# Channel-major weight products of a hybrid decoder trunk: rows' upper and lower parts in one 512-column matmul

## The chip, the cores and the metric

The kernel runs on one core of one Trainium2 chip. The metric is the time of one execution in device microseconds; before the change it is 1853.26 us, the median of three runs (1852.25 to 1854.35). Lower is better. Only matrix and vector work of one core is involved; there are no collectives.

## The reference, cut to what matters

Two decoder layers act on 256 rows of 1024 channels. Each layer has a token mixer (an RWKV-7 group of 8 heads and a native-sparse-attention group of 8 heads behind one input projection, then one output projection), a 4-head cross-attention into 256 memory rows, and a SwiGLU channel mixer: dense in layer 0, top-2 of 8 experts in layer 1. All arithmetic is float32.

```python
def rmsnorm(x, g):
    xf = x.astype(jnp.float32)
    y = xf * lax.rsqrt(jnp.mean(xf * xf, -1, keepdims=True) + NORM_EPS)
    return (y * g).astype(x.dtype)

def token_shift(u, mu):
    prev = jnp.pad(u, ((0, 0), (1, 0), (0, 0)))[:, :-1]
    return u + (prev - u) * mu

def cross_attention(h, m, wq, wkv, wo):
    q = (h @ wq).reshape(B, T, CROSS_HEADS, CROSS_HEAD_DIM)
    kv = (m @ wkv).reshape(B, M, 2, CROSS_HEADS, CROSS_HEAD_DIM)
    ...

def swiglu(h, wg, wu, wd):
    return (jax.nn.silu(h @ wg) * (h @ wu)) @ wd
```

The products that matter here are `h @ w` with h of 256 rows by 1024 channels: the mixer's input projection, the cross-attention's queries and keys, and the dense layer's gate and up products.

## The kernel before, in words

To keep float32 accuracy on the matrix engine, each operand is split into an upper part (rounded to the type float32r) and a lower part (what is left). A product is then three matmuls: upper by upper, lower by upper, upper by lower. Weights are split on the fly by `split` (L382 on ScalarE makes `wh`, L383 on VectorE makes `wl`), 128 by 1024 values at a time, into three rotating buffers in the mixers and more elsewhere.

`proj_b` (L396 to L410) makes channel-major results: 128 output channels on the partitions, 256 rows along the free dimension. A **tile** of weights from memory (1 MB, `raw`) has two **blocks** of 128 channels. For a block, the loop over 8 groups of input channels issues L405 (`wh` by the rows' upper part `hh`), L406 (`wh` by the lower part `hl`) and L407 (`wl` by `hh`), each 256 columns wide, all adding into one half of a PSUM bank. Both blocks of a tile share one bank, and the evicting function `evac` is called once for a tile. There are 120 blocks in the kernel, so 960 of each of the three matmuls:

- the mixer's RWKV columns, `proj_rwkv`, 14 blocks a layer; each block is evicted by `shift`, one ScalarE instruction (L580) and one VectorE instruction (L581) that both read PSUM;
- the mixer's attention columns, `proj_nsa`, 8 blocks a layer (`ev_c`, `ev_k`, `ev_q`);
- the memory's keys, `mem_kv`, 8 blocks a layer;
- the cross-attention's queries, `cross`, 8 blocks a layer;
- the dense layer's gate and up products, `dense`, 44 blocks. Here the results stay in PSUM until `second` multiplies them by 1 / rms (L1220, L1228).

`proj_a` (L424 to L426), `out_proj`, the dense down products (L1244 to L1246) and the experts (L1589 to L1591, L1628 to L1630) work row-major, with the weights as the 512-column moving operand; the change leaves them alone.

What sets the order of the work: each engine runs its own list of instructions, fixed when the program is built, by the order in the source, by readiness in the planner's estimate of times, and by a few edges written by hand (`behind`, `hold`, `chained`). In the mixer `weave` interleaves two lists of steps, RWKV's and the attention's with the memory's keys and values, by costs given with each `yield`. The PSUM banks of the tag `pj`, into which `proj_b` writes, are two in the mixer, three in the cross-attention and four in the dense layer. The experts (from about 850 us on) are written out in order by hand.

Of the kernel before, what the change touches and what calls it, by code (L numbers as in the profile page):

```python
# [14 lines left out]
D = 1024  # L15
# [20 lines left out]
M0 = 2, 1  # L36
# [121 lines left out]
def weave(*gens):  # L158
    """Steps of several generators, given as (generator, cost of all its steps), at an even pace."""
# [16 lines left out]
class Trunk:  # L176
# [37 lines left out]
    # constants  # L214
    def consts(self):
# [48 lines left out]
        # rows of a half of 32 in its second 16 and columns in its first  # L264
# [16 lines left out]
        # a pair of heads' sums go to rows 32 j and 32 j + 1, and to the two after those, which keep their lower parts  # L281
# [53 lines left out]
    # weights  # L335
# [24 lines left out]
    def extra(self, ctx, nraw, nspl, side=None):  # L360
        """Further buffers for the weights until ctx ends."""
# [34 lines left out]
    def proj_b(self, src, hh, hl, evac, tag="pj", m=128):  # L396
        """src [n, 128, 2, 8, 128]: channel-major blocks; evac(first block, psum [128, 2, 256])."""
        nc = self.nc
        for n in range(src.shape[0]):
            w, self.early = self.early or self.raw(src[n]), None  # L400
            ps = self.bank3(tag, 2)
            for b in range(2):
                wh, wl = self.split(w[:, b])
                for k in range(8):
                    nc.tensor.matmul(ps[:, b], wh[:, k], hh[:, k], start=(k == 0), stop=False)  # L405
                    nc.tensor.matmul(ps[:, b], wh[:, k], hl[:, k], start=False, stop=False)  # L406
                    nc.tensor.matmul(ps[:, b], wl[:, k], hh[:, k], start=False, stop=(k == 7))  # L407
# [41 lines left out]
    def rms(self, src, pool, junk, name="rs", both=False):  # L449
        """1 / rms of the rows: [128, 2]; junk [128, >= 512] is written over. Squares by ACT, or by DVE too."""  # L450
# [23 lines left out]
    def behind(self, ins, name):  # L474
        """The engine issues ins after the other of its instructions."""
# [1229 lines left out]
```

## Time and profile before

| | us |
|---|---|
| time, median of three runs | 1853.26 (1852.25 to 1854.35) |
| profiled execution, first to last instruction (span) | 1849.4 |
| median time less that span | 3.9 |
| TensorE busy in the span | 1808.4 |
| VectorE busy | 1461.3 |
| ScalarE busy | 1219.6 |

The profiled execution is one more execution; the page gives its span and not a time of its own, so the 3.9 us that lie around the span are taken from the median of the runs. In the rows, PE is TensorE's matmuls, PEld its weight loads, DVE VectorE, ACT ScalarE, POOL GpSimd. The end of a matmul is modelled, so the duration of one (283 ns for 256 columns) holds its latency; what a matmul costs in a stream is the distance from its start to the start of the next one.

### The profile page before, as it was taken

The page shows a single profiled execution, that of the slowest core. Times are in us where ns is not written, and L with a number is a line of the kernel's source. Part 1 is how long each engine was busy: PE and PEld are TensorE (multiplying, and loading weights), DVE is VectorE, ACT ScalarE, POOL GpSimd, SP SyncE. Part 2 cuts the span into 40 slices and gives each one's busy share as a digit, 9 for nine tenths or more (in the row PEclk, how much of TensorE's full clock was granted, in tenths as well). Part 3 has the DMA queues.
Part 4 walks back from the last instruction along what each step waited for, and adds up shares of the span by engine and source line. Part 5 has one row for each costly group of instructions (what it writes and reads, how often), then busy time and mean ns, then how long its engine had stood idle before and what let it go on. Part 6 is the DMA issues. An engine that isn't in the chain of part 4 may idle for free.

```text
span 1849.4 us, 28947 instructions
## 1 busy us (share of the span) xinstructions
PE 1808.4 (98%) x11309; PEld 1514.4 (82%) x11309; DVE 1461.3 (79%) x1947; ACT 1219.6 (66%) x1632; POOL 68.3 (4%) x152
## 2 busy tenths in 40 slices
PE   9999999999999999999999999999999999999997
PEld 9886788999988877877888788888888888888885
DVE  6777475655568774748999899998999999999997
ACT  7654354544466644448778677777777878777776
POOL 3100000000001100010000000000000000000000
PEclk9999999999999999999999999999999999999999
DMA  6532163555244421758998799998999989999990
GB/s 233 177 143 70 47 261 129 177 186 182 69 138 159 139 92 47 284 218 317 364 352 330 272 350 351 368 362 321 369 358 362 369 319 365 363 356 369 356 358 27
DMA packets 66674, 467.28 MB, mean 253 GB/s; under 512 B 7377, under 2 KB 7505, under 8 KB 11745
## 3 DMA queue, kind: packets, MB, share of 16 engines
q1 hardware_dynamic: 66208, 464.79, 68.5%
q8 instruction: 90, 1.47, 0.3%
q10 hardware_dynamic: 288, 0.52, 0.1%
q14 instruction: 56, 0.45, 0.1%
q0 software_dynamic: 32, 0.03, 0.0%
HBM read 464.27 MB, written 1.05 MB: 252 GB/s over the span
## 4 chain that ended last, share of the span: by engine, by line
PE 90%; DVE 5%; ACT 3%; issue 1%; DMA 0%; SPq 0%; ACTq 0%; DVEq 0%
PE gu L1591 11%; PE gu L1590 11%; PE gu L1589 11%; PE y L1629 6%; PE y L1628 6%; PE y L1630 6%; PE pj L405 6%; PE pj L406 6%; PE pj L407 6%; DVE wl L383 2%; PE pj L424 1%; PE pj L426 1%; PE pj L425 1%; PE tr L1605 1%; PE acc L1244 1%; PE acc L1245 1%
## 5 line engine op out<-in xcount | busy, mean ns | idle before, releaser
L383 DVE TENSOR_TENSOR wl<-raw,wh 128x1024 fp32r<-128x1024 f32 (+1 forms) x846 | 1019.7, 1218 | 191.2 <-ACT wh L382 185.0
L382 ACT CAST wh<-raw 128x1024 fp32r<-128x1024 f32 (+1 forms) x848 | 877.2, 1040 | 420.1 <-PE pj L406 142.2
L1589 PE MATMUL gu<-wh,xe 128*128 128x512 f32 x896 | 356.5, 398 | 0.0
L1591 PE MATMUL gu<-wh,xe 128*128 128x512 f32 x896 | 354.1, 395 | 0.0
L1590 PE MATMUL gu<-wl,xe 128*128 128x512 f32 x896 | 351.9, 393 | 0.0
L406 PE MATMUL pj<-hl,wh 128*128 128x256 f32 x960 | 276.3, 289 | 3.4 <-DVE hl L446 3.4
L407 PE MATMUL pj<-hh,wl 128*128 128x256 f32 x960 | 274.7, 287 | 1.4 <-DVE wl L383 1.4
L405 PE MATMUL pj<-hh,wh 128*128 128x256 f32 x960 | 275.3, 288 | 0.6 <-DVE gl L581 0.4
L1591 PEld LDWEIGHTS gu<-wh,xe 128*128 128x128 f32 x896 | 168.1, 188 | 38.5
L1590 PEld LDWEIGHTS gu<-wl,xe 128*128 128x128 f32 x896 | 168.6, 188 | 37.8
L1589 PEld LDWEIGHTS gu<-wh,xe 128*128 128x128 f32 x896 | 168.4, 188 | 35.6
L406 PEld LDWEIGHTS pj<-hl,wh 128*128 128x128 f32 x960 | 186.8, 195 | 6.1 <-DVE hl L446 4.5
L405 PEld LDWEIGHTS pj<-hh,wh 128*128 128x128 f32 x960 | 186.0, 194 | 4.5 <-issue 2.0
L407 PEld LDWEIGHTS pj<-hh,wl 128*128 128x128 f32 x960 | 186.8, 195 | 2.5 <-DVE wl L383 1.9
L1629 PE MATMUL y<-wl,hth 128*128 128x512 f32 x448 | 177.8, 397 | 2.4 <-DVE wl L383 2.4
L1628 PE MATMUL y<-wh,hth 128*128 128x512 f32 x448 | 178.4, 398 | 0.0
L1630 PE MATMUL y<-wh,htl 128*128 128x512 f32 x440 | 174.4, 396 | 0.0
L1629 PEld LDWEIGHTS y<-wl,hth 128*128 128x128 f32 x448 | 84.6, 189 | 22.7 <-DVE wl L383 2.9
L1628 PEld LDWEIGHTS y<-wh,hth 128*128 128x128 f32 x448 | 84.7, 189 | 19.9
L1630 PEld LDWEIGHTS y<-wh,htl 128*128 128x128 f32 x440 | 83.1, 189 | 20.1
L1601 DVE SCALAR_TENSOR_TENSOR h<-gu,gs,h 128x512 f32<-128x512 f32 x56 | 41.7, 744 | 1.7 <-ACT wh L382 0.9
L1065 ACT ACTIVATE pn<-pn,mx 128x128 f32<-128x128 f32 x64 | 28.5, 447 | 16.1 <-DVE mx L1062 15.7
(515 smaller groups left out, 2119.9 us busy)
## 6 DMA issues: line engine op xcount, KB each, us to landing
raw<-eg SPq DMA_DIRECT2D x106, 1024.0 KB, 5.1
raw<-eu SPq DMA_DIRECT2D x104, 1024.0 KB, 5.0
raw<-ed SPq DMA_DIRECT2D x104, 1024.0 KB, 5.2
raw<-win SPq DMA_DIRECT2D x21, 1024.0 KB, 4.9
raw<-dg SPq DMA_DIRECT2D x11, 1024.0 KB, 4.8
raw<-du SPq DMA_DIRECT2D x11, 1024.0 KB, 4.8
raw<-dd SPq DMA_DIRECT2D x11, 1024.0 KB, 4.8
raw<-ck SPq DMA_DIRECT2D x8, 1024.0 KB, 4.8
```

The costliest lines, as they stand in the source:

```text
L382: nc.scalar.copy(wh[:, c], w[:, c])
L383: (low or nc.vector).tensor_sub(wl[:, c], w[:, c], wh[:, c].bitcast(F32))
L405: nc.tensor.matmul(ps[:, b], wh[:, k], hh[:, k], start=(k == 0), stop=False)
L406: nc.tensor.matmul(ps[:, b], wh[:, k], hl[:, k], start=False, stop=False)
L407: nc.tensor.matmul(ps[:, b], wl[:, k], hh[:, k], start=False, stop=(k == 7))
L1589: nc.tensor.matmul(ps, xe[0][:, k + kk, es], wh[:, kk], start=(k + kk == 0), stop=False)
L1590: nc.tensor.matmul(ps, xe[0][:, k + kk, es], wl[:, kk], start=False, stop=False)
L1591: nc.tensor.matmul(ps, xe[1][:, k + kk, es], wh[:, kk], start=False, stop=(k + kk == 7))
L1601: nc.vector.scalar_tensor_tensor(h, gu[1], rs, h, op0=ALU.mult, op1=ALU.mult)
L1628: nc.tensor.matmul(ys[o], hh[:, k], wh[:, c], start=st, stop=False)
L1629: nc.tensor.matmul(ys[o], hh[:, k], wl[:, c], start=False, stop=False)
L1630: nc.tensor.matmul(ys[o], hl[:, k], wh[:, c], start=False, stop=sp)
```

## The change

Rows are held in one tile `hx` with the upper and the lower part of a channel group next to each other, 2 by 256 columns. In `proj_b` one 512-column matmul multiplies `wh` by both parts, and one of 256 columns multiplies `wl` by the upper part, into the first half of the bank. A block now fills a whole PSUM bank: its first half holds two of the three products, its second half the third. `evac` is called for every block, and the halves are added on the way out: `both` copies one half by ScalarE and adds the other by VectorE. What used to read PSUM afterwards (`shift`, the multiplications by 1 / rms) reads the result in SBUF. The hunks left out drop comments, follow the renaming, and join the two buffers `m1` and `m2` of the last layers into one of twice the size, `m12`.

```diff
-    def proj_b(self, src, hh, hl, evac, tag="pj", m=128):
-        """src [n, 128, 2, 8, 128]: channel-major blocks; evac(first block, psum [128, 2, 256])."""
+    def proj_b(self, src, hx, evac, tag="pj"):
...
             w, self.early = self.early or self.raw(src[n]), None
-            ps = self.bank3(tag, 2)
             for b in range(2):
+                ps = self.bank3(tag, 2)
                 wh, wl = self.split(w[:, b])
                 for k in range(8):
-                    nc.tensor.matmul(ps[:, b], wh[:, k], hh[:, k], start=(k == 0), stop=False)
-                    nc.tensor.matmul(ps[:, b], wh[:, k], hl[:, k], start=False, stop=False)
-                    nc.tensor.matmul(ps[:, b], wl[:, k], hh[:, k], start=False, stop=(k == 7))
-                if b:
-                    evac(2 * n, ps)
+                    nc.tensor.matmul(ps.rearrange("p a t -> p (a t)"), wh[:, k], hx[:, k].rearrange("p a t -> p (a t)"),
+                                     start=(k == 0), stop=False)
+                    nc.tensor.matmul(ps[:, 0], wl[:, k], hx[:, k, 0], start=False, stop=(k == 7))
+                evac(2 * n + b, ps)
                 yield 2.6

+    def both(self, dst, ps, scale=1.0):
+
+        self.nc.scalar.activation(dst, ps[:, 1], AF.Copy, scale=scale)
+        self.nc.vector.scalar_tensor_tensor(dst, ps[:, 0], scale, dst, op0=ALU.mult, op1=ALU.add)
+
...
-        hh = self.rw.tile([128, 8, 256], F32R, name="hh")
-        hl = self.rw.tile([128, 8, 256], F32R, name="hl")
+        hx = self.rw.tile([128, 8, 2, 256], F32R, name="hx")
+        hh, hl = hx[:, :, 0], hx[:, :, 1]
...
-        def ev_w(b, ps):
-            self.shift(ps[:, 0], 12, self.wa)
-            self.shift(ps[:, 1], 13, self.gl)
-
         def ev(dst, o):
             def f(b, ps):
-                for q in range(2):
-                    self.shift(ps[:, q], o + b + q, dst[:, b + q])
+                self.both(dst(b), ps)
+                self.shift(dst(b), o + b, dst(b))
             return f
...
-        def ev_c(b, ps):
-            for s in range(2):
-                for g in range(2):
-                    sl = slice(64 * g, 64 * g + 64)
-                    copy = nc.vector.tensor_copy if s else nc.scalar.copy
-                    copy(self.kv2[s][0:64, g], ps[sl, s])
-                    copy(self.kv2[s][64:128, g, 0:255], ps[sl, s, 1:256])
+        def ev_c(s, ps):
+            for g in range(2):
+                sl = slice(64 * g, 64 * g + 64)
+                for d, p in ((self.kv2[s][0:64, g], ps[sl]), (self.kv2[s][64:128, g, 0:255], ps[sl, :, 1:256])):
+                    nc.scalar.copy(d, p[:, 1])
+                    nc.vector.tensor_add(d, d, p[:, 0])

         def ev_k(b, ps):
-            nc.scalar.copy(self.ks[:, 16:272], ps[:, 0])
-            nc.scalar.copy(self.kw, ps[:, 1])
+            self.both(self.kw if b else self.ks[:, 16:272], ps)

         def ev_q(b, ps):
-            for i in range(2):
-                nc.scalar.activation(self.q[:, b + i], ps[:, i], AF.Copy, scale=self.qs[:, b + i:b + i + 1])
...
+            self.both(self.q[:, b], ps, self.qs[:, b:b + 1])
...
         def ev_k(b, ps):
-            nc.scalar.copy(kt[:, b:b + 2], ps)
+            self.both(kt[:, b], ps)
...
             if b == 0:
                 self.rb = self.rb()
-            nc.vector.scalar_tensor_tensor(q[:, b:b + 2], ps, 1.0 / 16, self.rb, op0=ALU.mult, op1=ALU.mult)
...
+            self.both(q[:, b], ps, 1.0 / 16)
+            nc.vector.tensor_mul(q[:, b], q[:, b], self.rb[:, 0])
...
         def first(s):
-            got = []
-            run(self.proj_b(a["dg"][s:s + 1], hh, hl, lambda b, ps: got.append(ps)))
-            run(self.proj_b(a["du"][s:s + 1], hh, hl, lambda b, ps: got.append(ps)))
+            got = [gp.tile([128, 2, 256], F32, name=n) for n in "gu"]
+            for m, t in zip(("dg", "du"), got):
+                run(self.proj_b(a[m][s:s + 1], hx, lambda b, ps: self.both(t[:, b], ps)))
             return got

         def second(s, got):
-            g = gp.tile([128, 2, 256], F32, name="g")
-            nc.vector.tensor_mul(g, got[0], self.rb)
+            g, u = got
+            nc.vector.tensor_mul(g, g, self.rb)
...
-            u = gp.tile([128, 2, 256], F32, name="u")
-            nc.vector.tensor_mul(u, got[1], self.rb)
+            nc.vector.tensor_mul(u, u, self.rb)
```

## Rows read from the trace of the kernel before

**Rows 1.** The page: busy time of each engine; TensorE's and VectorE's busy tenths in 40 equal slices of the span, with the granted clock; the chain that ended last, by engine.

```profile
PE 1808.4 (98%) x11309; PEld 1514.4 (82%) x11309; DVE 1461.3 (79%) x1947; ACT 1219.6 (66%) x1632; POOL 68.3 (4%) x152
...
PE   9999999999999999999999999999999999999997
...
DVE  6777475655568774748999899998999999999997
...
PEclk9999999999999999999999999999999999999999
...
PE 90%; DVE 5%; ACT 3%; issue 1%; DMA 0%; SPq 0%; ACTq 0%; DVEq 0%
```

**Rows 2.** Busy time of each engine by stage: everything ahead of the experts (0 to 850), layer 0's RWKV products (9.5 to 55), the first part of its weave (55 to 100), the whole weave (55 to 236), the cross-attention's queries (250 to 285), the dense layer (326 to 512.5), layer 1's weave (562 to 742). Columns: stretch in us, its length, busy us and count of PE, PEld, DVE, ACT and POOL, granted clock, DMA share, GB/s.

```profile
0.00:850.00 850.00, 823.77 (x6897) 714.39 (x6897) 543.25 (x1062) 445.42 (x791) 61.16 (x149) 0.99 0.44 155
9.50:55.00 45.50, 43.50 (x345) 42.43 (x344) 32.28 (x70) 32.28 (x55) 14.73 (x75) 0.96 0.61 218
55.00:100.00 45.00, 41.77 (x363) 38.90 (x362) 38.06 (x45) 29.47 (x50) 7.38 (x5) 0.96 0.50 167
55.00:236.00 181.00, 175.32 (x1871) 141.04 (x1870) 119.95 (x308) 93.48 (x198) 8.60 (x7) 0.98 0.29 102
250.00:285.00 35.00, 33.30 (x239) 31.57 (x237) 23.40 (x32) 18.86 (x30) 0.00 (x0) 0.95 0.84 335
326.00:512.50 186.50, 186.24 (x1316) 175.05 (x1316) 109.39 (x120) 86.49 (x103) 2.01 (x11) 1.00 0.44 148
562.00:742.00 180.00, 173.81 (x1882) 140.63 (x1881) 123.87 (x309) 95.39 (x202) 18.42 (x14) 0.99 0.30 103
```

**Rows 3.** What TensorE waited for ahead of the experts (0 to 850 us): its line, the releasing line, us in total, times, longest.

```profile
PE rw L647 <- DVE r L641: 5.7, 2, 2.9
PE pj L406 <- DVE hl L446: 3.4, 3, 1.3
...
PE pj L407 <- DVE wl L383: 1.4, 2, 0.8
```

**Rows 4.** TensorE in order of time in the dense layer, the first matmul of each of seven runs: 96 matmuls of 256 columns from each L405 row to the next L1244 row, 24 of 512 columns from each L1244 row to the next L405 row. Columns: start us, duration us, line, output and inputs, shape.

```profile
366.31 0.40 PE L1244 MATMUL acc<-wh,gh 128*128 128x512 f32 x1
...
371.76 0.28 PE L405 MATMUL pj<-hh,wh 128*128 128x256 f32 x1
...
383.20 0.40 PE L1244 MATMUL acc<-wh,gh 128*128 128x512 f32 x1
...
388.67 0.29 PE L405 MATMUL pj<-hh,wh 128*128 128x256 f32 x1
...
400.19 0.40 PE L1244 MATMUL acc<-wh,gh 128*128 128x512 f32 x1
...
405.73 0.28 PE L405 MATMUL pj<-hh,wh 128*128 128x256 f32 x1
...
417.24 0.39 PE L1244 MATMUL acc<-wh,gh 128*128 128x512 f32 x1
...
422.82 0.28 PE L405 MATMUL pj<-hh,wh 128*128 128x256 f32 x1
```

**Rows 5.** The first and the last of 22 matmuls of 256 columns whose weights are only 24 columns wide (L620 to L622, `tail`), in order of time, with the columns of rows 4.

```profile
31.77 0.28 PE L620 MATMUL rw<-hh,wh 128*24 128x256 f32 x1
...
34.15 0.28 PE L620 MATMUL rw<-hh,wh 128*24 128x256 f32 x1
```

**Rows 6.** The evicting and splitting instructions that are there before, groups by line with their shapes: the copy of 256 columns out of PSUM by ScalarE, the same with a scale per partition, the shift's two instructions, the copy of 64 partitions by VectorE, an addition of 256 columns by VectorE, the queries of two blocks in one instruction, and the two halves of a weight split. Rows with min/median/max in ns are from the views of the single lines; rows with "busy us, mean ns" from the list of groups.

```profile
L947 ACT COPY ks<-pj x2: 372/373/374, 73.7 to 581.4; 128x256 f32<-128x256 f32 x2
...
L952 ACT ACTIVATE q<-pj,qs x8: 462/467/474, 90.9 to 603.9; 128x256 f32<-128x256 f32 x8
...
L580 ACT ACTIVATE sh<-pj,vecs x28: 455/473/499, 21.4 to 568.1; 128x256 f32<-128x256 f32 x28
...
L581 DVE SCALAR_TENSOR_TENSOR big<-pj,omm,sh x16: 457/480/485, 26.4 to 569.1; 128x256 f32<-128x256 f32 x16
...
L943 DVE COPY vc<-pj x4: 417/422/427, 68.5 to 577.1; 64x256 f32<-64x256 f32 x4
...
L874 DVE TENSOR_TENSOR st<-st,pl x4: 418/418/426, 197.3 to 711.1; 128x256 f32<-128x256 f32 x4
...
L1158 DVE SCALAR_TENSOR_TENSOR q<-pj,rsb x8: 684/691/692, 269.5 to 788.0; 128x512 f32<-128x512 f32 x8
...
L383 DVE TENSOR_TENSOR wl<-raw,wh 128x1024 fp32r<-128x1024 f32 x199 | 244.8, 1231 | 132.1 <-ACT wh L382 131.1
...
L382 ACT CAST wh<-raw 128x1024 fp32r<-128x1024 f32 x202 | 211.3, 1047 | 239.6 <-PE pj L406 142.2 <-PE pj L426 35.9 <-PE acc L1246 21.9
```

**Rows 7.** One eviction of a tile in layer 0's RWKV products, ScalarE and then VectorE in order of time; in brackets the engine's idle time before and what ended it.

```profile
46.13 1.05 ACT L382 CAST wh<-raw 128x1024 fp32r<-128x1024 f32 x1 [1.66 <-issue]
47.09 0.47 ACT L580 ACTIVATE sh<-pj,vecs 128x256 f32<-128x256 f32 x1
48.87 0.47 ACT L580 ACTIVATE sh<-pj,vecs 128x256 f32<-128x256 f32 x1 [1.31 <-DVE vf L581]
...
47.21 1.23 DVE L383 TENSOR_TENSOR wl<-raw,wh 128x1024 fp32r<-128x1024 f32 x1 [1.25 <-ACT wh L382]
48.35 0.48 DVE L581 SCALAR_TENSOR_TENSOR vf<-pj,omm,sh 128x256 f32<-128x256 f32 x1
```

**Rows 8.** The matmul of layer 0's weave with TensorE's longest wait there, in order of time, with the columns of rows 7.

```profile
83.75 0.51 PE L647 MATMUL rw<-r,indt 128*128 128x256 f32 x2 [2.87 <-DVE r L641]
```

More of the change, by code (lines that the diff above doesn't have):

```diff
@@ L537, in mixer @@
         last = nc.cur_bb.bb.instructions[-1]
-        run(self.proj_rwkv(hh, hl))
+        run(self.proj_rwkv(hx))
         if l == 0:
@@ L547, in mixer @@
         run(weave((chain(self.rwkv_elem(), self.rwkv_chunks(), self.rwkv_out()), RC[l]),
-                  (chain(self.proj_nsa(hh, hl), take(mem, M0[l]), weave((self.nsa(), 32), (mem, 42 - 2.6 * M0[l]))), 95)))
+                  (chain(self.proj_nsa(hx), take(mem, M0[l]), weave((self.nsa(), 32), (mem, 42 - 2.6 * M0[l]))), 95)))
         run(self.out_proj(l))
@@ L595, in proj_rwkv @@
         win = a[f"win{l}"]
[L597 to L599 removed]
         def ev(dst, o):
             def f(b, ps):
[L603 to L611 removed]
+                self.both(dst(b), ps)
+                self.shift(dst(b), o + b, dst(b))
+            return f
+        yield from self.proj_b(win[0:1], hx, ev(lambda b: self.gl if b else self.wa, 12))
+        yield from self.proj_b(win[1:3], hx, ev(lambda b: self.k[:, b], 4))
+        self.tail(hx[:, :, 0], hx[:, :, 1])
+        yield from self.proj_b(win[3:5], hx, ev(lambda b: self.v[:, b], 8))
+        yield from self.proj_b(win[5:7], hx, ev(lambda b: self.r[:, b], 0))
     def tail(self, hh, hl):
@@ L967, in proj_nsa @@
         yield 5.2
-        yield from self.proj_b(win[9:11], hh, hl, ev_q)
+        yield from self.proj_b(win[9:11], hx, ev_q)
     def compress(self):
@@ L1134, in ev_k @@
         def ev_k(b, ps):
-            nc.scalar.copy(kt[:, b:b + 2], ps)
+            self.both(kt[:, b], ps)
         def ev_v(n, i, ps):
             nc.scalar.copy(vm[:, i, 512 * n:512 * n + 512], ps)
-        yield from self.proj_b(a[f"ck{l}"], mh, ml, ev_k)
+        yield from self.proj_b(a[f"ck{l}"], mx, ev_k)
         t = lambda s: (lambda k, i: s[:, k, 128 * i:128 * i + 128])
@@ L1157, in ev_q @@
                 self.rb = self.rb()
-            nc.vector.scalar_tensor_tensor(q[:, b:b + 2], ps, 1.0 / 16, self.rb, op0=ALU.mult, op1=ALU.mult)
-        run(self.proj_b(a[f"cq{l}"], hh, hl, ev_q))
-        oh, ol = (cp.tile([128, 8, 256], F32R, name=n, tag=t) for n, t in zip(("oh", "ol"), tags))
+            self.both(q[:, b], ps, 1.0 / 16)
+            nc.vector.tensor_mul(q[:, b], q[:, b], self.rb[:, 0])
+        run(self.proj_b(a[f"cq{l}"], hx, ev_q))
+        ox = cp.tile([128, 2, 8, 256], F32R, name="ox", tag=tags[0])
+        oh, ol = ox[:, 0], ox[:, 1]
         for h in range(4):
@@ L1269, in moe @@
         xl = self.xl = mo.tile([128, 2, D], F32R, name="xl")
-        temps = [self.op.tile([128, 2 * D], F32, name="more", tag=f"m{i}") for i in range(3)]
+        m12 = self.op.tile([128, 2, 2 * D], F32, name="more", tag="m12")
+        temps = [self.op.tile([128, 2 * D], F32, name="more", tag="m0"), m12[:, 0], m12[:, 1]]
         temps.append(x.rearrange("p i d -> p (i d)"))
@@ L1442, in gather @@
         yield gap and LOOK + 1
-        xp, ts = (self.op, ("m1", "m2")) if e0 % 4 else (mo, ("xeh", "xel"))
-        xe = [xp.tile([128, 8, 256], F32R, name="xe", tag=t) for t in ts]
+        if e0 % 4:
+            xe = self.op.tile([128, 2, 8, 256], F32R, name="xe", tag="m12")
+            xe = [xe[:, 0], xe[:, 1]]
+        else:
+            xe = [mo.tile([128, 8, 256], F32R, name="xe", tag=t) for t in ("xeh", "xel")]
         self.xe[e0 // 2] = xe
```

30 lines of the change are left out of this document (13 added, 17 removed).

## The prediction

> **What bounds the kernel now.** I read the page first. TensorE is busy in 98% of the span, at full clock in every slice, and nine tenths of the chain that ended last lie on it [rows 1]. Then I split the span by stage: ahead of the experts TensorE is idle for 850.0 - 823.8 = 26.2 us in all, and in the dense layer for 0.3 us of 186.5 [rows 2]. The waits of TensorE say the same: the longest group is 5.7 us in two waits, both for VectorE in the RWKV part [rows 3]. So each matmul's price counts nearly in full, and the rest of the question is whether what the change lays on ScalarE and VectorE stays hidden. A matmul's own duration doesn't tell its price, since neighbours overlap; the distance of starts does. In the dense layer three runs of 96 matmuls of 256 columns take 11.44, 11.52 and 11.51 us, so 119.2 to 120.0 ns each, mean 119.7; four runs of 24 of 512 columns take 5.45, 5.47, 5.54 and 5.58 us, so 227.1 to 232.5, mean 229.6 [rows 4]. At 2.4 GHz the columns alone would be 106.7 and 213.3 ns, so one matmul carries 13 to 16 ns that don't double with its width.
>
> **Removed: TensorE time.** For each group of input channels three matmuls of 256 columns become one of 512 and one of 256: from 3 x 119.7 = 359.1 to 229.6 + 119.7 = 349.3 ns, a gain of 9.8 ns. The kernel has 960 groups: 9.4 us. By stage that is 3.4 us in the dense layer (352 groups), 2.2 in the RWKV products (224), 2.5 in the attention columns and the memory's keys (256), 1.3 in the queries (128). No row shows a 512- and a 256-column matmul in turn on such operands. From the runs' ends the gain per group is at least 2 x 119.2 - 232.5 = 5.9 ns (5.7 us in all) and at most 2 x 120.0 - 227.1 = 12.9 ns (12.4 us). I take the mean. What half of the fixed part belongs to can be seen: with weights of 24 columns a 256-column matmul takes 2.38 us / 21 = 113.3 ns [rows 5], so 6.4 of the 13 ns go with the width of the weight load, and the change drops one load of three.
>
> A rule speaks against this gain. The Trainium skill (TensorE: Matmul & The Clock Gate, section Back-to-back issue gap) gives a warm matmul N / 2.4 plus 2.5 ns, so joining two would save 2.5 ns and the 960 groups 2.4 us. The rows have 13 ns over the columns at 256, not 2.5, in streams that load new weights each time; I go by the rows.
>
> **Added: evictions.** Every block now needs one ScalarE copy and one VectorE addition, and `shift` and the scalings come on top. Prices: a copy of 256 columns out of PSUM by ScalarE 373 ns, with a scale per partition 467; a VectorE instruction with a scalar and two tensors over 256 columns 480, over 64 partitions 422, a plain one 418; the queries' old one for two blocks 691 [rows 6].
>
> - VectorE: RWKV 28 x 0.48 = 13.4; `ev_c` 8 more x 0.42 = 3.4; `ev_k` 4 x 0.48 = 1.9; `ev_q` 8 x 0.48 = 3.8; memory's keys 16 x 0.48 = 7.7; queries 16 x (0.48 + 0.42) - 8 x 0.69 = 8.9; dense 44 x 0.48 = 21.1. Sum 60.2 us.
> - ScalarE: RWKV 28 x 0.373 = 10.4; `ev_c` 8 x 0.37 = 3.0; queries 6.0; dense 16.4; `ev_k` and `ev_q` nothing, since the copies were there; for the memory's keys 16 narrow copies stand for 8 wide ones, between 0 and 6.0, taken 3. Sum 38.8 us.
>
> How much of these 99 us reaches TensorE? Low bound: ahead of the experts 26.2 us of idle TensorE stand against 543.3 + 445.4 = 988.7 us of VectorE and ScalarE work [rows 2], 2.65%, so 2.6 us. High bound: the chain has 5% of the span on VectorE and 3% on ScalarE [rows 1], 92 and 55 us; if all of that lay ahead of the experts it would be 17% and 12.5% of their busy time there, so 10.2 + 4.9 = 15.1 us. Spread over their work in the whole span it is 6.3% and 4.5%, so 3.8 + 1.8 = 5.6 us. I take 5.6, and the stages agree with it:
>
> - The dense layer takes the most and pays nothing: VectorE goes from 109.4 to 130.5 us of 186.5, ScalarE from 86.5 to 103 [rows 2]. Four banks now turn once a block, and the matmuls of the step before stand between a step's last eviction and its use: 24 of them, 5.5 us [rows 4], which cover about 4 x 0.69 + 0.48 + 0.37 = 3.6 us. Without that cover each of 11 steps would pay some of it.
> - The weave pays the most. From 55 to 100 us VectorE is already at 38.1 of 45 us [rows 2] and gets two RWKV blocks, `ev_c`, `ev_k` and `ev_q`, 1.0 + 1.7 + 1.0 + 1.9 = 5.6 us. Its largest wait, L647 for L641, 2.87 us [rows 8], ends a chain over both engines; what is queued ahead of it there makes it longer, and the weight splits behind it late, for which the next block waits. Between 0 and 5.6 us a layer; I take 2, so 4 of the 5.6.
> - RWKV products and queries share the remaining 1.6 us.
>
> **Moved.** The first 512-column matmul needs the lower part of the rows, so one matmul (0.12 us) that could run ahead of it no longer can. L406 waited for `hl` three times, 3.4 us [rows 3]. Five stage starts stand open (two mixers, two cross-attentions, the dense layer): 0.6 us. No transfer is added or moved in a queue. Joining `m1` and `m2` costs nothing that I can see: both halves served the same stage; the experts hide it under 980 us of full TensorE, and if the cover fails a gather waits once.
>
> **Sum.** -9.4 + 5.6 + 0.6 = -3.2 us: span 1849.4 to 1846.2, and with the 3.9 us around it, to the median, 1850.1 us.
>
> **Rivals.**
>
> 1. All evictions stay hidden as well as today's work: -9.4 + 2.6 + 0.6 = -6.2, so 1847.1 us. For it: 26 us of idle TensorE in 850, and VectorE at 64% there [rows 2]. Against it: the crowded stretch from 55 to 100 us.
> 2. It ends slower: the two `pj` banks of the mixer become the bound in the RWKV products. Today ScalarE splits weights first, at 46.13, and evicts after, because the weights' buffer comes free a matmul before the block ends; the addition on VectorE stands behind the `wl` split and ends at 48.83 [rows 7]. That is 2.7 us after the release, in a bank that used to have two blocks' time and now has one, 8 x 0.349 = 2.79 us. If the order of instructions then puts the shift's ScalarE instruction (0.47) ahead of the next split, a block turns every 2.7 + 0.1 + 0.47 = 3.3 us: 0.5 us too slow. With all 28 blocks that is +14, of which 1 is in the sum: +10, so 1863 us; with half of them 1857 us. From about 14 blocks on the kernel is slower by more than can be taken for no change. Against it: ScalarE's work for a block is 1.05 + 0.37 + 0.47 = 1.9 us and VectorE's 2.2, and an order that evicts first costs nothing.
> 3. The pair gains only the low end, 5.7 us, because a wide matmul takes 232.5 ns while transfers run: -5.7 + 6.2 = +0.5, so 1853.8 us. By the rule above it would be -2.4 + 6.2 = +3.8, 1857 us.
>
> **Chances.** Forecast (part given back, 1848 to 1853 us) 0.42; rival 1 0.28; rival 2 0.18; rival 3 0.12. A difference of 0.2%, 3.7 us, is about what a measurement of this kernel can tell from no change. Faster by more: rival 1, and the lower third of the forecast, 0.42. Within: the rest of the forecast and most of rival 3, 0.37. Slower: rival 2 and the tail of 3, 0.21. The range for 8 in 10 runs from 1844.5 (the high gain of 12.4 less 2.6 and 0.6 would be 1844.1) to 1858.5 (rival 2 with half the blocks, and a little more); the forecast's own is 1848 to 1853.
>
> **What would show it.** Right: from start to start a wide and a narrow matmul of `proj_b` take about 349 ns together; the dense layer is 3.4 us shorter with TensorE still full; the gain is smaller or negative from 55 to 100 us, with a longer wait at L647's place; VectorE has some 60 us more, ScalarE 39. Wrong: pairs at 357 ns or more (rival 3); waits of `proj_b`'s first matmul for the VectorE half of `both` (rival 2); a static order of matmuls in the weave that came out otherwise and moved more than all the terms here.

## The result, and the profile after

The changed kernel takes 1862.83 us, the median of five runs (1861.96 to 1866.44), against 1853.26 (1852.25 to 1854.35) before: the ratio is 1.0053 with a 95% interval of 1.0037 to 1.0068. It is 9.6 us slower. The forecast was 1850.1 us and its range ended at 1858.5, so both the sign and the size were missed. The profiled execution of the changed kernel took 1862.83 us, with a span of 1861.0.

First the page of the changed kernel, the lines that answer to [rows 1]: busy times, the granted clock in 40 slices, and the chain that ended last.

```profile
PE 1803.7 (97%) x10349; PEld 1461.6 (79%) x10349; DVE 1503.2 (81%) x2079; ACT 1250.5 (67%) x1736; POOL 65.0 (3%) x152
...
PEclk9999899999999999999999999999999999999999
...
PE 88%; DVE 7%; ACT 3%; issue 1%; POOL 0%; DMA 0%; SPq 0%; DVEq 0%; ACTq 0%; POOLq 0%
```

TensorE is busy 4.7 us less, and yet the span is 11.6 us longer. VectorE's share of the chain has gone from 5 to 7%, and one slice of the clock row is no longer at 9. So time was added in which TensorE stands, or runs slowly. What it waited for ahead of the experts (0 to 860 us; line, releasing line, us in total, times, longest), which answers to [rows 3]:

```profile
PE pj L406 <- DVE kc L945: 11.8, 2, 6.0
PE pj L406 <- DVE hx L451: 4.5, 4, 1.5
PE pj L406 <- DVE wa L415: 3.9, 2, 2.3
...
PE pj L406 <- DVE kt L415: 2.5, 1, 2.5
PE pj L408 <- DVE wl L383: 1.8, 3, 1.1
...
PE pj L962 <- DVE ks L415: 1.4, 2, 1.1
```

L406 is now the 512-column matmul of `proj_b`, L408 the narrow one, L414 and L415 the two instructions of `both`, L944 and L945 those of `ev_c`. The longest wait of before, for `r`, 5.7 us in two [rows 3], is gone, and a wait of twice that size has come: L406 for L945, the last addition of `ev_c` on the compress keys, once in each layer. The waits for `wa`, `kt` and `ks` are new too. In all four a first matmul finds no empty bank (L962 is the first of the attention's values, which use the same two banks).

The saving itself is there. TensorE in order of time in the dense layer, which answers to [rows 4]: 64 matmuls from each L406 row to the next L1244 row (32 wide, 32 narrow).

```profile
376.42 0.39 PE L406 MATMUL pj<-hx,wh 128*128 128x512 f32 x1
...
387.68 0.40 PE L1244 MATMUL acc<-wh,gh 128*128 128x512 f32 x1
...
393.13 0.40 PE L406 MATMUL pj<-hx,wh 128*128 128x512 f32 x1
...
404.39 0.40 PE L1244 MATMUL acc<-wh,gh 128*128 128x512 f32 x1
```

11.26 us for 32 groups are 351.9 ns a group; five such runs take 11.13 to 11.28 us, a mean of 351.1, against 359.1 before and 349.3 forecast (the expectations below reckon with 351.6).

**Where the time went.** To add up a whole trace I read windows of 1 us from 9 us to the first matmul of the experts, and put each into three parts: TensorE idle; TensorE busy but at a lower granted clock (busy time times one minus the clock); and the rest, work at full clock. The table has all kernels of this study; the experts behind that point are the same in each. "Ratio" is the time against the kernel before on the same chip, with its 95% interval; it is estimated from all runs of both, so it need not be the quotient of the two medians given below. One run each of e9_four_banks (6140.66 us) and e13_dv_on_vector (2145.31 us) fell in a slower state and is left out.

| kernel | ratio | idle us | lower clock us | work us |
|---|---|---|---|---|
| before | 1 | 24.3 | 11.8 | 794.7 |
| changed | 1.0053 (1.0037 to 1.0068) | 40.6 | 18.0 | 785.7 |
| e1_evc_once | 0.9997 (0.9985 to 1.0009) | 28.9 | 14.7 | 790.4 |
| e5_old_kcvc | 1.0006 (0.9995 to 1.0018) | 30.4 | 11.9 | 790.5 |
| e2_old_mixer | 0.9985 (0.9972 to 0.9998) | 25.1 | 13.4 | 791.3 |
| e7_kcvc_alone | 1.0045 (1.0027 to 1.0062) | 31.3 | 20.6 | 789.3 |
| e6_three_pj | 1.0087 (1.0064 to 1.0110) | 37.6 | 31.1 | 786.7 |
| e3b_evict_only | 1.0124 (1.0105 to 1.0142) | 41.7 | 19.7 | 796.3 |
| e8_rwkv_new | 0.9979 (0.9964 to 0.9994) | 27.4 | 15.0 | 789.2 |
| e9_four_banks | 0.9995 (0.9983 to 1.0008) | 32.4 | 18.5 | 786.1 |
| e10_banks_once | 0.9995 (0.9976 to 1.0014) | 28.3 | 25.1 | 786.0 |
| e11_rwkv_banks | 0.9937 (0.9921 to 0.9954) | 24.8 | 6.8 | 789.2 |
| e12_kcvc_old_banks | 0.9982 (0.9971 to 0.9992) | 25.6 | 15.2 | 788.6 |
| e4_half_mixer | 0.9962 (0.9949 to 0.9975) | 28.4 | 13.4 | 786.8 |
| e13_dv_on_vector | 0.9976 (0.9959 to 0.9993) | 26.6 | 11.9 | 789.1 |
| e14_banks_dv_vector | 0.9953 (0.9936 to 0.9970) | 24.0 | 13.6 | 788.7 |

From before to changed: work -9.0, idle +16.3, lower clock +6.2, together +13.5 at the experts' first matmul (the experts then give 1.9 back). Of the idle time +6.1 and +5.7 lie in the two weaves, and of the lower clock +5.3 and +6.0. The three parts come from one execution of each kernel, and the lower clock is the least steady of them: 29 timed runs of the kernel before on one chip reach from 1850.28 us at a mean clock of 0.992 to 1859.57 at 0.986. Of the changed kernel's 18.0 us at the lower clock 1.8 and 2.6 lie behind the two waits for `kc`; 10.2 lie in three stretches, from 202, 229 and 738 us on, ahead of which TensorE had not been idle for 7 us, and what set those off is not shown. Work is not exact either: the changed kernel, e1, e9, e10 and e4 have the same matmuls and stand at 785.7 to 790.4.

**How the wait of 6 us comes about.** The eviction of the compress keys in layer 0 of the changed kernel, each engine in order of time (TensorE, ScalarE, VectorE; start us, duration us, line, output and inputs, in brackets the idle time before and what ended it).

```profile
65.23 0.40 PE L406 MATMUL pj<-hx,wh 128*128 128x512 f32 x1
...
65.58 0.40 PE L406 MATMUL pj<-hx,wh 128*128 128x512 f32 x1
...
72.67 0.76 PE L406 MATMUL pj<-hx,wh 128*128 128x512 f32 x1 [6.01 <-DVE kc L945]
...
73.45 0.63 PE L406 MATMUL pj<-hx,wh 128*128 128x512 f32 x1
...
74.09 0.63 PE L406 MATMUL pj<-hx,wh 128*128 128x512 f32 x1
...
64.26 0.35 ACT L944 COPY kc<-pj 64x256 f32<-64x256 f32 x1
64.51 1.05 ACT L382 CAST wh<-raw 128x1024 fp32r<-128x1024 f32 x1
65.46 1.06 ACT L701 ACTIVATE big<-big 128x1024 f32<-128x1024 f32 x1
66.54 0.36 ACT L944 COPY kc<-pj 64x255 f32<-64x255 f32 x1
...
67.31 1.28 ACT L690 ACT_TABLE_LOAD   x1
...
69.02 0.37 ACT L944 COPY kc<-pj 64x256 f32<-64x256 f32 x1
...
70.87 0.37 ACT L944 COPY kc<-pj 64x255 f32<-64x255 f32 x1
...
65.53 0.41 DVE L945 TENSOR_TENSOR kc<-kc,pj 64x256 f32<-64x256 f32 x1
65.86 1.21 DVE L383 TENSOR_TENSOR wl<-raw,wh 128x1024 fp32r<-128x1024 f32 x1
67.10 0.42 DVE L945 TENSOR_TENSOR kc<-kc,pj 64x255 f32<-64x255 f32 x1
...
70.32 1.75 DVE L694 RECIPROCAL s<-s 128x256 f32<-128x256 f32 x1
72.10 0.42 DVE L945 TENSOR_TENSOR kc<-kc,pj 64x255 f32<-64x255 f32 x1
```

Eight instructions of some 0.4 us each, 3.1 us of work, are spread from 64.26 to 72.52. Each addition needs its own copy, and between the copies stand a weight split, an activation, a table load of 1.28 us; between the additions a split, a reciprocal of 1.75 us. Both lists are fixed, so nothing overtakes. From the first copy to the last addition the bank is held for all of the 8.3 us; the other bank holds the compress values; the third block waits from 66.66 to 72.67. The price is also paid behind the wait: 65.23 to 65.58 is 0.35 us from wide to wide matmul, 73.45 to 74.09 is 0.64. The windows of the same stretch (us, length, busy us and count of PE, PEld, DVE, ACT, POOL; granted clock; DMA share, GB/s):

```profile
62.00:66.00 4.00, 4.00 (x24) 3.31 (x22) 1.78 (x4) 3.99 (x5) 1.26 (x1) 1.00 0.63 246
66.00:72.60 6.60, 0.67 (x9) 0.16 (x8) 5.77 (x11) 6.40 (x13) 0.00 (x0) 0.76 0.48 160
72.60:77.00 4.40, 4.33 (x15) 3.78 (x16) 4.34 (x7) 1.19 (x4) 0.56 (x1) 0.58 0.00 0
```

TensorE had the upper of its two levels, 2.4 GHz, until it stood idle; it came back at the lower, 1.2 GHz, and ran five groups so (in layer 1 eight, behind a wait of 5.84 us). The Trainium skill (TensorE: Matmul & The Clock Gate, section A second HAM failure mode: psum-queue depth-cycling) tells of a kernel whose idling between groups, as it went through its PSUM banks, let the clock fall and recover again and again; these rows show one such fall, with one wait of 6.01 us.

### The profile page after: what moved, and what is told of

It is laid out like the page before. It is cut to its first block, busy times and chain, and to the rows that moved or that the text cites. A ratio compares the mean times of both kernels' runs of the same rounds, so it can differ in the third digit from the quotient of the medians.

```text
span 1861.0 us, 27261 instructions
## 1 busy us (share of the span) xinstructions
PE 1803.7 (97%) x10349; PEld 1461.6 (79%) x10349; DVE 1503.2 (81%) x2079; ACT 1250.5 (67%) x1736; POOL 65.0 (3%) x152
## 4 chain that ended last, share of the span: by engine, by line
PE 88%; DVE 7%; ACT 3%; issue 1%; POOL 0%; DMA 0%; SPq 0%; DVEq 0%; ACTq 0%; POOLq 0%
PE gu L1595 11%; PE gu L1594 11%; PE gu L1593 11%; PE pj L406 10%; PE y L1633 6%; PE y L1632 6%; PE y L1634 6%; PE pj L408 5%; DVE wl L383 2%; PE pj L429 1%; PE pj L430 1%; PE pj L431 1%; PE tr L1609 1%; PE acc L1244 1%; PE acc L1246 1%; PE acc L1245 1%
## 5 line engine op out<-in xcount | busy, mean ns | idle before, releaser
L406 PE MATMUL pj<-hx,wh 128*128 128x512 f32 x960 | 348.9, 405 | 23.8 <-DVE kc L945 11.8
L1594 PE MATMUL gu<-wl,xe 128*128 128x512 f32 x896 | 351.9, 393 | 0.0
L408 PE MATMUL pj<-hx,wl 128*128 128x256 f32 x960 | 273.0, 285 | 1.8 <-DVE wl L383 1.8
L406 PEld LDWEIGHTS pj<-hx,wh 128*128 128x128 f32 x960 | 183.1, 191 | 72.6 <-issue 15.0
L408 PEld LDWEIGHTS pj<-hx,wl 128*128 128x128 f32 x960 | 184.1, 192 | 5.2 <-DVE wl L383 2.8
L1633 PEld LDWEIGHTS y<-wl,hth 128*128 128x128 f32 x448 | 84.2, 188 | 22.5 <-DVE wl L383 2.9
L1632 PEld LDWEIGHTS y<-wh,hth 128*128 128x128 f32 x448 | 84.3, 188 | 19.7
L1605 DVE SCALAR_TENSOR_TENSOR h<-gu,gs,h 128x512 f32<-128x512 f32 x56 | 41.7, 745 | 1.7 <-ACT wh L382 0.9
L1604 ACT ACTIVATE h<-gu,gs 128x512 f32<-128x512 f32 x56 | 38.1, 680 | 0.0
L1616 DVE TENSOR_TENSOR htl<-tr,hth 128x512 fp32r<-128x512 f32 x55 | 37.7, 685 | 0.1
```

The source lines that it names most:

```text
L406: nc.tensor.matmul(ps.rearrange("p a t -> p (a t)"), wh[:, k], hx[:, k].rearrange("p a t -> p (a t)"), start=(k == 0), stop=False)
L408: nc.tensor.matmul(ps[:, 0], wl[:, k], hx[:, k, 0], start=False, stop=(k == 7))
L1594: nc.tensor.matmul(ps, xe[0][:, k + kk, es], wl[:, kk], start=False, stop=False)
L1604: nc.scalar.activation(h, gu[0], AF.Silu, scale=rs)
L1605: nc.vector.scalar_tensor_tensor(h, gu[1], rs, h, op0=ALU.mult, op1=ALU.mult)
L1632: nc.tensor.matmul(ys[o], hh[:, k], wh[:, c], start=st, stop=False)
```

## The experiments

Theory A: `ev_c` alone is the cause, because it holds a bank for 8 us. Theory B: the evictions as a whole are too many for ScalarE and VectorE. Theory C: TensorE's saving is too small.

**Compress keys and values evicted once (e1_evc_once).**

```diff
         def ev_c(s, ps):
+            t = self.vt[:, s]
+            self.both(t, ps)
+            copy = nc.vector.tensor_copy if s else nc.scalar.copy
...
-                    nc.scalar.copy(d, p[:, 1])
-                    nc.vector.tensor_add(d, d, p[:, 0])
+                copy(self.kv2[s][0:64, g], t[sl])
+                copy(self.kv2[s][64:128, g, 0:255], t[sl, 1:256])
```

> Compress keys and values of the NSA mixer: each block is taken off its PSUM bank by two instructions (one copy, one add, into a scratch tile in SBUF), and the four placing copies read SBUF afterwards; everything else is as in the changed kernel. Theory A (the bank of the compress keys is held for 8.3 us by eight alternating instructions in two in-order queues, the next block has no bank, and TensorE idles 6 us and then runs some 4 us at the lower clock, in each layer): the waits of 6.0 and 5.8 us in front of the selection keys' block go to 1 to 2 us, and the time falls by 8 to 14 us, to 1849 to 1855. Theory B (evictions in two instructions are too many for ScalarE and VectorE in the weave, wherever they are, and what is freed here waits at the next bank): the wait only moves, and the time stays within 3 us of the changed kernel's, 1860 to 1863. Theory C (TensorE's own saving is too small, the waits cost little): no change, 1862 to 1863.

Measured: 1853.78 us against 1855.81 before on the same chip, 0.9997 of it. TensorE's waits ahead of the experts in this kernel:

```profile
PE pj L406 <- DVE hx L451: 4.5, 4, 1.5
PE rw L648 <- DVE r L642: 4.1, 2, 2.3
PE pj L406 <- DVE wa L415: 3.8, 2, 2.3
```

No wait for `kc` is left, and the wait for `r` of before is back (L642). The bank is free after two instructions. Six of them are left for a block in place of eight, so this run alone does not part the bank from the instructions; the four banks below, which keep all eight, do. Theory A holds for some 10 us; B in its plain form and C fall.

**Compress keys and values in the old form (e5_old_kcvc).** The old `proj_b` under the name `proj_old`, for one tile of the mixer.

```diff
-        yield from self.proj_b(win[7:8], hx, ev_c)
+        yield from self.proj_old(win[7:8], hh, hl, ev_c)
```

> Compress keys and values alone (32 of the 960 groups of matmuls) go back to the old form: three 256-column matmuls, one bank for both blocks, eight copies that need no partner. All else is as in the changed kernel. Theory A: the 6.0 and 5.8 us waits disappear, and with them the time at the lower clock; the time falls by 10 to 16 us, to 1847 to 1853. Theory B: 1859 to 1863, the stall coming back at the selection keys or at the queries. Theory C: 1862 to 1863.

Measured: 1856.59 us, 1.0006 of before. The waits for `kc` and the time behind them go, as A says; but the time is above the 1853 us at which A's range ended, and the kernel does not come out below the one before, so what its matmuls save (7.4 us at 8.0 ns for each of 928 groups, 4.2 in the table) is spent elsewhere.

**The whole mixer in the old form (e2_old_mixer).** `proj_old` and the old evictions in `proj_rwkv`, `proj_nsa` and `mem_kv`.

> Old matmuls and old evictions in all of the mixer (RWKV products, NSA columns, memory keys); the new form is left in the cross queries and the dense product alone. Theory A and theory B both say that the dense stage keeps its 2.4 us and the queries some 1 us, with no loss in the mixer: 1849 to 1851. Theory C: within 1 us of the kernel before, 1852 to 1854.

Measured: 1852.32 us, 0.9985 of before, 2.8 us less. The dense layer is 2.4 us shorter, as in the changed kernel. So the change pays where TensorE's neighbours have time, and by about what the matmuls save there.

**The new form for the compress keys and values alone (e7_kcvc_alone).** The kernel above, with the one tile new.

```diff
-        yield from self.proj_old(win[7:8], hh, hl, ev_c)
+        yield from self.proj_b(win[7:8], hx, ev_c)
```

> The counterpart of the run that took the compress keys and values back: the mixer is old in all but the compress keys and values, which alone (32 of the mixer's 512 groups of matmuls) have the new form with its eviction in eight alternating instructions; queries across and the dense product stay new. Theory A (this eviction is the cause): a wait of 5 to 6 us in front of the selection keys in each layer, time at the lower clock behind it, and a time 8 to 14 us above that of the kernel with the old mixer, which is 6 to 11 us above the kernel before. Theory B (the evictions of the whole mixer together): at most 3 us above the kernel with the old mixer, so not above the kernel before.

Measured: 1862.06 us, 1.0045 of before, so 0.60% or 11 us above the kernel with the old mixer. Its longest wait:

```profile
PE pj L420 <- DVE kc L966: 11.3, 2, 5.6
```

L420 is the old form's first matmul: the next block, old as it is, waits for the same bank. 32 groups of 960, which save some 0.3 us of matmuls, cost these 11 us; the changed kernel as a whole lost 9.6. With e1 and e5 this settles the two long waits.

**Three banks for the projections, two for RWKV (e6_three_pj).**

```diff
-        self.psum(mc, f"pm{l}", {"rw": 3, "pj": 2, "ns": 2, "pv": 1})
+        self.psum(mc, f"pm{l}", {"rw": 2, "pj": 3, "ns": 2, "pv": 1})
```

> The changed kernel with three banks for the projections and two for the RWKV part (three before), all else the same. Theory A: the selection keys take the third bank, so that the waits of 6.0 and 5.8 us fall below 2 us; where the RWKV part does well with two banks the time is 1848 to 1855. If the RWKV part needs its third bank, waits for it appear under its own lines, and the time says nothing on the theory, but the rows of the selection keys do. Theory B: the eviction queues are the limit, and with a bank more the stall only comes a block later, 1859 to 1863.

Measured: 1871.47 us, 1.0087 of before. The wait for `kc` is gone; in its place come waits for `wl` (6.9 us in five), for `ks` (3.7), and in the RWKV part for `rk` (3.8) and `kbt` (3.0). The RWKV part needs its third bank, so the time says little on the cause.

**Evictions without the saving (e3b_evict_only).**

```diff
-                    nc.tensor.matmul(ps.rearrange("p a t -> p (a t)"), wh[:, k], hx[:, k].rearrange("p a t -> p (a t)"),
-                                     start=(k == 0), stop=False)
+                    nc.tensor.matmul(ps[:, 1], wh[:, k], hx[:, k, 1], start=(k == 0), stop=(k == 7))
+                for k in range(8):
+                    nc.tensor.matmul(ps[:, 0], wh[:, k], hx[:, k, 0], start=(k == 0), stop=False)
                     nc.tensor.matmul(ps[:, 0], wl[:, k], hx[:, k, 0], start=False, stop=(k == 7))
```

> The new banks and evictions, with TensorE's work of the kernel before: each group is three 256-column matmuls (the lower rows' half first, then the upper half) in place of one of 512 and one of 256. It measures the evictions without the saving. By the pitches of the dense stage (359.1 ns for three, 351.6 ns for the pair) the saving is 960 x 7.5 ns = 7.2 us where TensorE never waits, so theories A and B both give the changed kernel's time plus the part of 7.2 us that is on the path, 1865 to 1870. Theory C (the pair saves next to nothing): 1862 to 1864.

Measured: 1876.88 us, 1.0124 of before, 13 us above the changed kernel by the ratios and above the 1865 to 1870 expected. The work column says 10.6 us of it, where 960 groups at 8.0 ns make 7.7. Part of the rest is this order's own, since a block now begins with the lower part of the rows: L406 waits 9.0 us for `hx`, against 4.5 in the changed kernel. The saving is real and lies on the path; theory C falls.

**Four banks (e9_four_banks).** The second block of a pair takes one of the two banks of NSA's scores.

```diff
-                ps = self.bank3(tag, 2)
+                ps = self.bank3(tag[b], 2)
...
-        yield from self.proj_b(win[7:8], hx, ev_c)
+        yield from self.proj_b(win[7:8], hx, ev_c, ("pj", "ns"))
```

> The changed kernel, but the second block of each pair takes one of the two banks of NSA's scores, which stand empty then, in the RWKV products and in the NSA columns: four banks for the projections, and the RWKV part keeps its three. Theory A in its narrow form (the wait is for a bank alone): the waits of 6.0 and 5.8 us in front of the selection keys are gone, the waits of 2.3 us for wa too, and the time falls by 10 to 16 us to that of the kernel before or 4 us below it. Theory A in its wide form (the eight alternating instructions hold VectorE's and ScalarE's queues as well, and the splits of the next weights stand behind them): the wait moves to the split or to a later block, and no more than half of it, 5 us, is won. The run with three banks, which took one of the RWKV part's, speaks for the wide form, but it had losses of its own.

Measured: 1854.83 us, 0.9995 of before. No wait for a projection's bank is among its longest any more, and the time falls by 0.58%, 11 us. Of the 7.2 us that the profiled execution has gained at the experts' first matmul, 2.5 are in layer 1's RWKV products, where the wait for `wa` is gone, and only 2.8 and 2.1 in the weaves, which had lost 8.7 and 11.1. There the wide form holds; that the whole time fell by 11 us is what the narrow form said. Of this kernel the waits for `wl`, then the largest of layer 0's weave with VectorE and GpSimd ahead of it:

```profile
PE pj L408 <- DVE wl L383: 11.6, 6, 3.9
...
81.69 0.58 PE L408 MATMUL pj<-hx,wl 128*128 128x256 f32 x1 [3.32 <-DVE wl L383]
...
74.86 3.46 DVE L714 TENSOR_TENSOR kb<-big 64x1024 f32<-64x1024 f32 x1
78.35 0.42 DVE L945 TENSOR_TENSOR vc<-vc,ns 64x255 f32<-64x255 f32 x1
78.80 1.75 DVE L694 RECIPROCAL s<-s 128x256 f32<-128x256 f32 x1
80.47 1.16 DVE L383 TENSOR_TENSOR wl<-raw,wh 128x1024 fp32r<-128x1024 f32 x1
...
74.67 2.57 POOL L723 TENSOR_TENSOR rk<-big 128x1024 f32<-128x1024 f32 x1 [9.62 <-DVE big L706]
```

With a bank to write to, TensorE now waits for the weights' lower part, which stands on VectorE behind the last addition of `ev_c`, a reciprocal, and a product that took 3.46 us in place of 1.22 when GpSimd had started 0.19 us earlier (the last section has more on this).

**Both cures (e10_banks_once).** The four banks and e1's `ev_c`.

> The four banks of the run beside this one, and the compress keys and values taken off their banks by two instructions before they are placed from SBUF: both cures at once. Narrow form of theory A: no better than the four banks alone within 2 us. Wide form: 5 us or more below the four banks alone. In both, the saving of the RWKV products (1.1 us a layer) grows by the waits for wa that go (1.6 to 2.3 us a layer), so that the time lies 0 to 5 us below the kernel before.

Measured: 1853.89 us, 0.9995 of before, the same as either alone. The narrow form's number came out, but not for its reason: the idle time is 4.1 us less than with the banks alone, and the lower clock takes 6.6 us more in the profiled execution, which with 1859.52 us was one of the slower ones of this kernel.

**New form in the RWKV products, the queries and the dense layer only (e8_rwkv_new).** `proj_old` and the old evictions in `proj_nsa` and `mem_kv`.

> The new form in the RWKV products, the queries across and the dense product; the old matmuls and evictions in what runs beside the RWKV recurrence (NSA columns and memory keys). By the trace of the changed kernel these stages gain 1.1, 2.5 and 0.3, 2.4 us and, in layer 1, 0.2 us, while the stretch beside the recurrence should be as before: theory A and B give 3 to 6 us below the kernel before on the same chip. If the new evictions of the RWKV products (wa 2.3 us) cost more than their matmuls save, it comes out no faster than the kernel with all of the mixer old.

Measured: 1850.43 us, 0.9979 of before, 3.9 us less, within what was expected. The waits for `wa` stay (4.1 us in two).

**The same with four banks in the RWKV products (e11_rwkv_banks).**

> The fastest form so far (new matmuls in the RWKV products, the queries across and the dense product, old ones beside the recurrence), with the four banks in the RWKV products alone. The waits of 2.3 and 1.8 us in front of the third block, for the bank of wa, should go: 2 to 4 us less than without, which makes 5 to 8 us below the kernel before on the same chip. If the shift of the first rows on VectorE is the true limit there, the wait moves to the next block and the time stays.

Measured: 1844.40 us against 1854.09 before on the same chip, 0.9937 (0.9921 to 0.9954), the fastest of all, 0.4% below the kernel without the banks by the ratios. Its waits:

```profile
PE rw L663 <- DVE r L657: 5.7, 2, 3.0
PE pj L406 <- DVE hx L466: 4.4, 5, 1.2
PE rw L462 <- DVE xs L549: 2.9, 1, 2.9
```

These are the waits of before [rows 3]; the four us for `wa` are gone. Against e8 the profiled execution has 2.6 us less idle time and 8.2 us less at the lower clock; the timed runs, whose median clock rose from 0.990 to 0.9915, show less of the second.

**All new but the compress keys and values, with four banks in the RWKV products (e12_kcvc_old_banks).**

> The compress keys and values alone have the old matmuls and evictions, all else the new form, and the RWKV products have four banks. It stands against the fastest kernel so far (four banks, and the old form in all that runs beside the recurrence, 0.9937 of the kernel before) by the other evictions beside the recurrence alone: selection and window keys, NSA's queries, memory keys. If the compress keys and values are the whole loss beside the recurrence, it is as fast or up to 2 us faster, since these matmuls save some 2 us. If the other evictions cost there too (waits for kt 2.5, for ks 1.4, for q 1.1 us, and time at the lower clock), it is 3 to 8 us slower than that kernel, 0.995 to 0.998 of the kernel before.

Measured: 1851.76 us, 0.9982 of before, 0.45% above e11. So the new form of the other products beside the recurrence costs too, some 8 us, where their matmuls should save 2. In layer 0's weave this kernel is 2.0 us faster than e11, in layer 1's 10.1 us slower, 8.5 of it at the lower clock. Layer 1 of this kernel, a wait with VectorE and GpSimd ahead of it, and the window behind it:

```profile
593.59 0.39 PE L408 MATMUL pj<-hx,wl 128*128 128x256 f32 x1 [1.85 <-DVE wl L383]
...
590.94 4.86 DVE L383 TENSOR_TENSOR wl<-raw,wh 128x1024 fp32r<-128x1024 f32 x3
...
590.10 2.35 POOL L750 TENSOR_TENSOR dv<-vf,v 128x1024 f32<-128x1024 f32 x1 [3.44 <-PE rw L648]
...
595.00:606.00 11.00, 11.00 (x73) 7.70 (x72) 4.39 (x10) 4.53 (x10) 4.84 (x3) 0.53 0.70 274
```

Three splits take 4.86 us and not 3.7, while GpSimd is at its subtraction until 592.45; TensorE waits 1.85 us and then runs 11 us at half the clock. The same wait of 1.85 to 2.1 us stands in e1, e5 and e10.

**First half evicted alone (e4_half_mixer).** The changed kernel, with only the first half of each bank evicted in the mixer, so that one of the three products is left out of the result there.

> The new matmuls everywhere and two banks, but in the mixer only the first half of each bank is evicted, with the instructions of the kernel before; the second half, the product of the weights' upper part with the rows' lower part, is left out of the result there. TensorE's work is that of the changed kernel, ScalarE's and VectorE's in the mixer that of the kernel before. If the evictions are the whole loss, the saving of TensorE stands alone: the waits for kc, wa, kt and q go, and the time is 8 to 10 us below the kernel before on the same chip, 0.995 of it. If it is the smaller bank of one block (a block has one bank of two to itself, and the next but one waits for it) whatever its eviction, the waits remain in part and the time is near that of the kernel before.

Measured: 1847.49 us against 1854.10, 0.9962, 7 us less. The waits for `kc`, `kt` and `q` go, and the one for `wa` stays at its size:

```profile
PE pj L406 <- DVE wa L586: 4.1, 2, 2.4
```

So with the evictions as short as before the change would have gained 7 us, and the wait for `wa` comes from the bank that lasts for one block, not from the instructions that the change adds.

**The subtraction on VectorE (e13_dv_on_vector, and its control e14_banks_dv_vector).**

```diff
-            nc.gpsimd.tensor_sub(d, self.vf, v)
+            nc.vector.tensor_sub(d, self.vf, v)
```

> The kernel with the compress keys and values alone in the old form and four banks for the RWKV products; layer 1's subtraction dv (2.35 us on GpSimd) is moved to VectorE (about 1.2 us there), all else the same. Theory D (VectorE's split of the next weights stands still while GpSimd subtracts, TensorE waits 1.85 us for it and runs at the lower clock behind that): the wait for wl at its place goes, the split takes 1.2 us again, and the time falls by 3 to 8 us, to 0.994 to 0.997 of the kernel before. Theory E (the other evictions themselves, or the order that the planner makes of them, cost the time): at most 1 us less, 0.998 of the kernel before.

> Control: the same move of dv in the kernel with four banks and the old form beside the recurrence, which has no such wait. Theory D and theory E both: within 2 us of that kernel, 0.993 to 0.995 of the kernel before. If it is faster by more, the move has a worth of its own and the run beside this one says less.

Measured: 1850.24 us, 0.9976 of before, where the kernel it was made from had 0.9982; the control 1844.94, 0.9953, where e11 had 0.9937. The wait for `wl` is gone, as theory D says, and the time has moved by 1 us, as E says. This does not decide between them: with the intervals of the table the move could be worth anything from 5 us less to 3 us more, and the control came out 3 us slower than e11 by the ratios, not within the 2 us expected. What can be seen is a new wait a few us later, for ScalarE, with some 7 us at the lower clock behind it:

```profile
PE rw L766 <- ACT kbt L768: 1.8, 1, 1.8
```

At an equal mean clock of 0.991 this kernel and its control still differ, 1848.2 against 1844.9 us (means of two runs each). What these 3 to 8 us of the other evictions are, one by one, stays open; no single wait carries them.

## Why the prediction was wrong, by its own steps

- **Removed work, -9.4.** Near: the work column fell by 9.0, and 960 groups at the measured 8.0 ns (9.8 forecast) make 7.7 us. The dense layer gave 2.4 us and not 3.4. By the estimate weighed in the prediction, from the formula of the Trainium skill (TensorE: Matmul & The Clock Gate, section Back-to-back issue gap), the pair would have gained 2.5 ns; the page gives that formula for a matmul by itself, and in these streams each matmul follows a weight load. The measured 8.0 ns lie between.
- **Evictions that reach TensorE, +5.6. This step failed.** Idle time rose by 16.3 and time at the lower clock by 6.2, 22.5 in all, above its high bound of 15.1 too. The bounds were shares: so much more work on two engines, so much more idle time of TensorE. `ev_c` stood there as 1.7 us of VectorE work. Its price was the time it holds a bank, 8.3 us, which no busy time tells: it follows from how many instructions alternate between two ordered lists and from what stands between them. The weave was put at 2 us a layer; it lost 8.7 and 11.1.
- **The clock was left out.** I took full clock throughout, though a 9 in a slice only says 90% or more, and three windows of before have 0.95 or 0.96 [rows 2]. Each wait was priced at its length; the waits of 6 us cost some 2 us more behind them.
- **Rival 2, at 0.18, had the right mechanism in the wrong place.** It saw that a bank lasts for one block and no longer two, and put the loss on every block of the RWKV products. There it cost one wait a layer, 2.3 and 1.6 us, for `wa`; the loss was at `ev_c`, whose eight instructions the prediction added up and did not lay out in the engines' order. Its sign, `proj_b`'s first matmul waiting for VectorE's addition, was seen, with `ev_c`'s addition in the place of that of `both`. That its 1863 us for all 28 blocks is also the measured time is chance: the two stages of these blocks came out 1.1 and 0.2 us shorter than before.
- **Dense layer pays nothing: right** (four banks; its idle time went from 3.1 to 3.5 us). **Stage starts +0.6: about right**, the waits for the rows' lower part went from 3.4 to 4.5 us.
- **L647's wait grows: wrong.** It vanished, since TensorE came there later (80.03 us in layer 0) than `r` was done (73.43).
- **VectorE +60, ScalarE +39:** the page has +41.9 and +30.9, but it counts a moment once in which two instructions of an engine overlap, as the rows above do by some 0.1 us. By the instructions' own durations it is +54.1 and +39.5. ScalarE was right; VectorE's addition takes 0.42 us where no scale per partition is applied, not 0.48.
- **Rival 1** gave -6.2 us for evictions that stay hidden; the run with halved evictions in the mixer had -7.0 by its ratio.

## What to carry to other kernels

Price an eviction by how long it holds its bank, not by its busy time: lay out the copies and additions in the order of both engines' lists, with what stands between them, and compare the sum with the time until that bank is next wanted. If a result must be scattered, take it off PSUM in as few instructions as possible and scatter from SBUF; where banks stand empty in a stage, lend them to the one that turns faster. And count a wait of TensorE at more than its length, as the clock may be at its lower level behind it.

## What was not expected of the hardware

**Products of two tensors on VectorE and GpSimd exclude each other.** In the four-bank kernel VectorE's product of two tensors, 1.22 us otherwise, took 3.46 us from 74.86 on, and GpSimd's ran from 74.67 to 77.24: it took as long as if it had begun at 77.10, when GpSimd's was ending. The other order is seen before: there VectorE had two such instructions from 74.38 to 76.73, and GpSimd's product, issued at 74.50, took 4.54 us in place of 2.45. The Trainium skill (SBUF — State Buffer, section SBUF: two separate sides) says that the two share a pair of ports by a lock, which a VectorE instruction with two inputs in SBUF takes against a GpSimd one that reads SBUF, and that whoever starts first keeps it for the whole instruction; the rows agree, with 2.24 and 2.09 us of standing still. In the changed kernel the order has turned against VectorE: its four products of this kind take 9.4 us in all, 4.9 before. What this adds to the loss was not tested.

**A wait of 2 us can cost more than its length again.** Waits of 1.85 us (e12) and of 1.8 (e13) were followed by 11 and some 7 us at the lower level, which cost 5.1 and 3.4 us; but of e11's two waits for `r`, that of 2.70 us was followed by some 4 us at the lower level and that of 3.00 by none, and there are falls without such a wait, as those of the changed kernel at 202, 229 and 738 us. So the clock is a cost with a large chance in it, and times of kernels that differ by 0.2% need many runs, compared at an equal clock.
